# The second group's output product by seven quarter products, feature-major, with sums of weights on GpSimd

## The chip, the cores and the metric

The kernel runs on one core of a Trainium2 chip. Its engines each run their own stream of instructions in order: TensorE (PE in the profile, its loads of stationary operands PEld), VectorE (DVE), ScalarE (ACT), GpSimd (POOL) and SyncE (SP, which issues nearly all transfers between HBM and SBUF). Matrix products go to PSUM, which has eight banks here: five under the tag "acc", three under "mix". The metric is the device time of one execution in microseconds (us), the median of several.

## What is computed

The reference is one layer of a bidirectional encoder, applied to a sample of 1024 tokens and a prompt of 256 with the same weights (D_MODEL 2048):

```python
hn = rms_norm(x, norm_g)
proj = hn @ w_in                                   # conv input, gates z, dt, q, k, v, mq
xbc = silu(centred_dwconv(xbc, conv_w, conv_b))
y = y_forward + y_backward + d_skip * xs           # SSD scans, chunks of 128, both directions
o_ssd = rms_norm over 2 groups of 512 (y * silu(z_ssd)), times ssd_norm_g
o_att = window_attention(q, k, v, sink) * silu(z_att)     # 512 features
o_mem = attention over 256 memory rows * silu(z_mem)      # 512 features
return x + concat([o_ssd, o_att, o_mem]) @ w_out          # 2048 x 2048
```

The last line is what the change is about. All data are float32.

## The kernel before

**Tiles and groups.** The 1280 tokens are ten tiles of 128, in two groups of five (group 0: tiles 0 to 4, group 1: tiles 5 to 9). For one group all activations that a product needs stay in SBUF, turned so that features lie on the partitions: four "quads" `xH0..3` and `xL0..3`, each 4 x 128 features by 640 tokens. Each float32 operand is held as a rounded part (H, or h for weights) and the rest (L, l), and a product is three matmuls: H h, H l and L h.

**Blocks.** `block_tok` computes 512 output columns for five token tiles: for each of 16 slices k of the contraction, SP loads 128 x 512 weights into `wraw` (four buffers), `wsplit` makes `wh` on ACT (L233, or L236 with a scale) and `wl` on DVE (L234 or L237), three buffers each; then come five token tiles x three matmuls (L285 to L287) with the activations stationary and 512 weight columns moving. The last two steps are merged, so that each token tile finishes early and is evacuated while the others run. `block_feat` (L320 to L322) is the other form: weights stationary, 320 tokens moving, the result has features on the partitions. The order of all blocks is written out at the end of the kernel function.

**Lanes.** All other work (attention, memory attention, SSD scans, norms) is written as generators in two queues, `lanes`. After every step of a block, `pump` takes as many steps of each lane as `RATES` says; `need` forces steps that something waits for. The framework then orders the instructions of each engine by priority and readiness, near this order; `high_priority` moves weight splits and evacuations ahead.

**SSD.** `ssd_up` goes through the tiles in ascending order and leaves a part of the result in DRAM; `ssd_down` goes in descending order (7 to 0, later 9 and 8), adds the backward part, multiplies with the gate (L1002), stores the product token-major (L1003, `o_d`), sums its squares on ACT (L1004), and gets the norm's factor on GpSimd (L135, L136, L1010) into `rs_all`.

**Output product.** The quads are refilled with the mixers' results by `refill_o`: quads 0 and 1 (attention, memory) straight from turned copies in DRAM (`oT_d`, by `fill_direct`, L217 to L227), quads 2 and 3 (SSD) by `fill_transposed` (L199 to L211), which loads a token tile, scales it with `rs_all` (L204), turns it by four transposes on TensorE (L207) and splits it (L210, L211). Fills use the three "ch" buffers. Then `block_tok` runs four blocks of 512 columns for group 0 (the lanes finish during the first three; the refill for group 1 runs during the fourth), and four for group 1. The norm's gain per feature rides on the weight splits of the last eight slices (L236, L237). `ev_out` adds the input rows (L416) and stores them (L417). During the last four blocks both lanes are empty.

## Time and profile before

| what | us |
|---|---|
| median of three runs | 1856.73 (1856.13 to 1857.54) |
| the profiled execution | 1857.13 |
| its span | 1855.4 |
| DVE busy in the span | 1068.2 |
| ACT busy | 776.0 |
| GpSimd busy | 84.6 |

The span reaches from the first to the last recorded instruction of one execution; 1.7 us of that execution lie around it. A busy time is the sum over an engine's instructions; matmuls overlap each other, so what one matmul costs in a stream is the distance between two starts, not its duration. A row of a group gives its line, engine, operation, output and inputs, count, then busy us and mean ns of one, then the idle time before it and what ended that. Lines are those of the kernel above.

### The profile page before, as it was taken

To read this page: it belongs to the slowest core of one execution; us is meant where nothing else is said; L and a number is where in the kernel's file an instruction comes from. 1 tells how busy PE (TensorE), PEld (TensorE's weight loads), DVE (VectorE), ACT (ScalarE), POOL (GpSimd) and SP (SyncE) were. 2 spreads that over 40 slices of the span, in tenths; PEclk is the share of its full clock that TensorE was granted. 3 is DMA by queue.
4 is the path that set the end of the run, shared out by engine and by line. 5 is a ranking of instruction groups with operands and counts; after the bars stand their busy time and mean duration, and the time that the engine had idled before them with its cause. 6 is when DMAs were issued, how large, how long until landed. Compare 5 with 4: busy or idle time off the path is not lost.

```text
span 1855.4 us, 28398 instructions
## 1 busy us (share of the span) xinstructions
PE 1847.1 (100%) x10402; PEld 1628.6 (88%) x10402; DVE 1068.2 (58%) x2156; ACT 776.0 (42%) x1753; POOL 84.6 (5%) x147
## 2 busy tenths in 40 slices
PE   9999999999999999999999999999999999999999
PEld 8889999998998889999989988777888888888887
DVE  5434555767456566668786665666885554342222
ACT  6553333434533655324335445544463442322121
POOL 0011001000000000000000000001100000000000
PEclk9999999999999999999999999999999999999999
DMA  8674444443432564533445445467775574554442
GB/s 290 234 234 126 121 148 142 130 123 95 137 128 87 165 200 133 146 96 116 123 140 162 135 142 175 116 214 253 233 218 158 150 228 133 177 173 136 133 123 69
DMA packets 191340, 289.39 MB, mean 156 GB/s; under 512 B 18977, under 2 KB 68193, under 8 KB 191201
## 3 DMA queue, kind: packets, MB, share of 16 engines
q1 hardware_dynamic: 191056, 287.53, 50.2%
q8 instruction: 82, 1.34, 0.3%
q14 instruction: 58, 0.47, 0.1%
q10 hardware_dynamic: 144, 0.06, 0.0%
HBM read 230.59 MB, written 56.92 MB: 155 GB/s over the span
## 4 chain that ended last, share of the span: by engine, by line
PE 94%; DMA 2%; ACT 1%; DVE 1%; issue 1%; SPq 0%; POOL 0%; ACTq 0%; DVEq 0%
PE acc L285 17%; PE acc L287 17%; PE acc L286 17%; PE acc L320 10%; PE acc L321 10%; PE acc L322 10%; PE py L923 2%; PE po L671 1%; PE ppt L661 1%; PE pmo L772 1%; PE pyb L998 1%; PE psc L629 1%; PE pyf L856 1%; PE psc L630 1%; DMA chd<-in_x_turned_dram 1%
## 5 line engine op out<-in xcount | busy, mean ns | idle before, releaser
L285 PE MATMUL acc<-wh,xH 128*128 128x512 f32 (+1 forms) x1568 | 609.6, 389 | 0.6 <-DVE zs L336 0.6
L287 PE MATMUL acc<-wh,xL 128*128 128x512 f32 (+1 forms) x1568 | 597.4, 381 | 0.0
L286 PE MATMUL acc<-wl,xH 128*128 128x512 f32 (+1 forms) x1568 | 596.2, 380 | 0.2 <-DVE wl L234 0.2
L234 DVE TENSOR_TENSOR wl<-wraw,wh 128x512 fp32r<-128x512 f32 (+1 forms) x416 | 278.5, 670 | 383.2 <-ACT wh L233 378.2
L233 ACT ACTIVATE wh<-wraw 128x512 fp32r<-128x512 f32 (+1 forms) x416 | 255.4, 614 | 581.7 <-PE acc L287 294.4
L320 PE MATMUL acc<-xH,wh 128*128 128x320 f32 x1280 | 402.7, 315 | 0.0
L322 PE MATMUL acc<-xH,wl 128*128 128x320 f32 x1280 | 396.1, 309 | 0.0
L321 PE MATMUL acc<-xL,wh 128*128 128x320 f32 x1280 | 395.6, 309 | 0.0
L285 PEld LDWEIGHTS acc<-wh,xH 128*128 128x128 f32 x1568 | 295.0, 188 | 57.7 <-issue 5.6
L286 PEld LDWEIGHTS acc<-wl,xH 128*128 128x128 f32 x1568 | 294.7, 188 | 56.2 <-issue 3.6
L287 PEld LDWEIGHTS acc<-wh,xL 128*128 128x128 f32 x1568 | 294.4, 188 | 55.8 <-issue 0.2
L320 PEld LDWEIGHTS acc<-xH,wh 128*128 128x128 f32 x1280 | 240.4, 188 | 5.4 <-issue 5.0
L321 PEld LDWEIGHTS acc<-xL,wh 128*128 128x128 f32 x1280 | 240.4, 188 | 2.0 <-issue 1.7
L322 PEld LDWEIGHTS acc<-xH,wl 128*128 128x128 f32 x1280 | 240.3, 188 | 0.4 <-issue 0.2
L237 DVE SCALAR_TENSOR_TENSOR wl<-wraw,vec,wh 128x512 fp32r<-128x512 f32 x64 | 48.1, 751 | 139.7 <-ACT wh L236 135.4
L236 ACT ACTIVATE wh<-wraw,vec 128x512 fp32r<-128x512 f32 x64 | 46.3, 723 | 134.1 <-PE acc L287 123.7
L394 DVE SCALAR_TENSOR_TENSOR c<-u,vec,c 128x638 f32<-128x638 f32 (+1 forms) x96 | 84.5, 880 | 0.7
L644 ACT ACTIVATE lg<-lg,nm 128x384 f32<-128x384 f32 (+1 forms) x80 | 45.0, 563 | 46.0 <-DVE nm L638 45.8
L906 ACT ACTIVATE rb<-rb,wj_all 128x128 f32<-128x128 f32 x160 | 52.7, 391 | 25.9 <-DMA rb<-ac 25.9
L227 DVE SCALAR_TENSOR_TENSOR xL<-chd,vec,xH 128x640 fp32r<-128x640 f32 (+1 forms) x48 | 39.7, 838 | 36.5 <-ACT xH L226 35.1
L631 DVE SCALAR_TENSOR_TENSOR lg<-ndist,psc 128x384 f32<-128x384 bf16 (+1 forms) x80 | 38.6, 495 | 27.4 <-PE psc L630 26.9
L906 ACT ACTIVATE rf<-rf,wj_all 128x128 f32<-128x128 f32 x160 | 52.1, 391 | 2.3 <-DMA rf<-ac 2.3
(254 smaller groups left out, 1762.2 us busy)
## 6 DMA issues: line engine op xcount, KB each, us to landing
wraw<-in_w_in_laid_dram SPq DMA_DIRECT2D x288, 256.0 KB, 2.8
wraw<-in_w_out_laid_dram SPq DMA_DIRECT2D x128, 256.0 KB, 2.8
chd<-in_x_turned_dram SPq DMA_DIRECT2D x32, 320.0 KB, 4.6
rf<-ac SPq DMA_DIRECT2D x40, 256.0 KB, 3.8
rb<-ac SPq DMA_DIRECT2D x40, 256.0 KB, 4.0
out_dram<-yt SPq DMA_DIRECT2D x40, 256.0 KB, 3.5
wraw<-in_w_mem_laid_dram SPq DMA_DIRECT2D x32, 256.0 KB, 4.3
xst<-in_x_sample_dram SPq DMA_DIRECT2D x32, 256.0 KB, 4.2
```

Source lines behind the costliest of these rows:

```text
L233: a = A.activation(h, raw, AF.Copy)
L234: b = V.tensor_sub(l, raw, h.bitcast(F32))
L236: a = A.activation(h, raw, AF.Copy, scale=g)
L237: b = V.scalar_tensor_tensor(out=l, in0=raw, scalar=g, in1=h.bitcast(F32), op0=ALU.mult, op1=ALU.subtract)
L285: T.matmul(ps[t][:, :n], sh, h[:, :n], start=(k_ == 0), stop=False)
L286: T.matmul(ps[t][:, :n], sh, l[:, :n], start=False, stop=False)
L287: T.matmul(ps[t][:, :n], sl, h[:, :n], start=False, stop=(k_ == KT - 1))
L320: T.matmul(o, sh, cur["H", q][:, m, c], start=(k == 0), stop=False)
L321: T.matmul(o, sh, cur["L", q][:, m, c], start=False, stop=False)
L322: T.matmul(o, sl, cur["H", q][:, m, c], start=False, stop=(k == KT - 1))
L394: V.scalar_tensor_tensor(out=c[:, :n], in0=u[:, k:k + n], scalar=cw[k], in1=c[:, :n], op0=ALU.mult, op1=ALU.add)
L906: A.activation(r[:, c], r[:, c], AF.Identity, bias=wj_all[:, t, h:h + 1])
```

## The change

Group 0 keeps its four blocks. For group 1, the product (2048 output features x 2048 x 640 tokens) is cut in halves along each of the three directions, and the eight quarter products are replaced by seven, with sums of quarters on both sides (`seven` names for each product which of four weight slices or four weight sums it uses, and which of seven token slices or sums). The result is feature-major and leaves the kernel as a second output of 2048 x 640, turned on the host. In detail:

- `block_pair(u)`, u = 0 to 7, makes 128 features of each half of the output: eight steps k, each with one load of four 128 x 128 weight quarters, four sums of them on GpSimd, two splits (384 and 512 columns), and seven products of three matmuls with 320 moving columns. The seven accumulators take five "acc" banks and two "mix" banks. The last two steps are merged.
- `fill_seven(k)` makes the seven token operands of one slice: two loads, one scaling by the norm's gain (on ACT), four subtractions on GpSimd, and three splits. For k from 4 to 7 they lie where the quads were, once group 0's last block is through with them (`free`).
- `ev_pair` adds the seven products into two output rows of 640 tokens, with nine additions on DVE and one copy on ACT.
- `ssd_down` now scales its product and turns it itself (four transposes, a copy on ACT, a store into `oT_d`), in four more steps of the lane. So `refill_o` takes all four quads by `fill_direct`, with the gain for the SSD quads, and the weight splits of the output product have no scale.
- The tiles that only the earlier stages use lie in two pools (`cl`, `mp`) that are closed ahead of group 0's fourth block, after the lanes have been emptied; the new pool `fin` takes their place.
- The rates of lane 1 are raised for z0, z1, mq, zm and o, that of lane 0 for o.

```diff
-         {'kv': (1.0, 1.0), 'x': (0.9, 1.05), 'q': (1.3, 2.3), 'za': (1.3, 2.3), 'z0': (1.5, 2.4), 'z1': (1.5, 2.4),
-          'mq': (1.5, 1.8), 'zm': (1.5, 1.8), 'o': (1.5, 1.65)})
+         {'kv': (1.0, 1.0), 'x': (0.9, 1.05), 'q': (1.3, 2.3), 'za': (1.3, 2.3), 'z0': (1.5, 2.5), 'z1': (1.5, 2.5),
+          'mq': (1.5, 2.7), 'zm': (1.5, 2.7), 'o': (1.55, 1.9)})
...
-    mp = ctx.enter_context(tc.tile_pool(name="mp", bufs=2))
     sm = ctx.enter_context(tc.tile_pool(name="sm", bufs=2))
+
+    beside = ExitStack()
+    cl = beside.enter_context(tc.tile_pool(name="cl", bufs=1))
+    mp = beside.enter_context(tc.tile_pool(name="mp", bufs=2))
...
+    def lconst(shape, name, dtype=F32):
+        return cl.tile(shape, dtype, tag=name, name=name)
...
-    kT = const([P, 2, 7 * P], "kT", F32R)
-    kL = const([P, 2, 7 * P], "kL", F32R)
-    v_all = const([P, 7, P], "v_all")
-    dt_all = const([P, NT, 32], "dt_all")
-    eacs_all = const([P, NT, 32], "eacs_all")
-    cd_all = const([P, NT, 32], "cd_all")
-    wj_all = const([P, NT, 32], "wj_all")
-    dd_all = const([P, NT, 32], "dd_all")
-    rs_all = const([P, NT, 2], "rs_all")
+    kT = lconst([P, 2, 7 * P], "kT", F32R)
+    kL = lconst([P, 2, 7 * P], "kL", F32R)
...
-    o_d = [[dram([P, 512], f"o{c}_{t}") for c in range(2)] for t in range(NT)]
-    oT_d = [[dram([P, 4, 640], f"oT{c}_{g}") for g in range(2)] for c in range(2)]
+    oT_d = [[dram([P, 4, 640], f"oT{c}_{g}") for g in range(2)] for c in range(4)]
...
-    def fill_transposed(q, i, src, scale=None):
-
-        ch = rp.tile([P, 640], F32, tag="ch", name="ch", bufs=CH)[:, :512]
-        last_load[0] = S.dma_start(ch, src)
-        yield
-        if i == 0:
-            new_quad(q)
-        if scale is not None:
-            V.tensor_scalar(out=ch, in0=ch, scalar1=scale, scalar2=None, op0=ALU.mult)
-        ps = psum("pr")
-        for j in range(4):
-            T.transpose(ps[:, j * P:(j + 1) * P], ch[:, j * P:(j + 1) * P], ident)
-        ps3 = hv(ps, 4)
-        h = cur["H", q][:, :, i * P:(i + 1) * P]
-        A.activation(h, ps3, AF.Copy)
-        V.tensor_sub(cur["L", q][:, :, i * P:(i + 1) * P], ps3, h.bitcast(F32))
-        yield
...
-    def wsplit(raw, h, l, g=None):
-        if g is None:
-            a = A.activation(h, raw, AF.Copy)
-            b = V.tensor_sub(l, raw, h.bitcast(F32))
-        else:
-            a = A.activation(h, raw, AF.Copy, scale=g)
-            b = V.scalar_tensor_tensor(out=l, in0=raw, scalar=g, in1=h.bitcast(F32), op0=ALU.mult,
-                                       op1=ALU.subtract)
+    def wsplit(raw, h, l):
+
+        a = A.activation(h, raw, AF.Copy)
+        b = V.tensor_sub(l, raw, h.bitcast(F32))
...
-        return w_laid(w_out_laid[c], 512, lambda k: vec[:, R_SG + k - 8:R_SG + k - 7] if k >= 8 else None)
+        return w_laid(w_out_laid[c], 512)
...
-            S.dma_start(o_d[t][g], y)
...
-        rsqrt(rs_all[:, t, :], ss, 1.0 / 512, 2)
-        G.tensor_scalar(out=rs_all[:, t, :], in0=rs_all[:, t, :], scalar1=rxh[:, t:t + 1], scalar2=None, op0=ALU.mult)
-        yield
+        rs = sm.tile([P, 2], F32, tag="s2", name="yrs", bufs=4)
+        rsqrt(rs, ss, 1.0 / 512, 2)
+        G.tensor_scalar(out=rs, in0=rs, scalar1=rxh[:, t:t + 1], scalar2=None, op0=ALU.mult)
+        yield
+        yield
+        for g in range(2):
+            y = ld[g][0]
+            V.tensor_scalar(out=y, in0=y, scalar1=rs[:, g:g + 1], scalar2=None, op0=ALU.mult)
+        yield
+        for g in range(2):
+            y = ld[g][0]
+            ps = psum("pr")
+            for j in range(4):
+                T.transpose(ps[:, j * P:(j + 1) * P], y[:, j * P:(j + 1) * P], ident)
+            o = mp.tile([P, 512], F32, tag="rf", name="so", bufs=2)
+            A.activation(o, ps, AF.Copy)
+            S.dma_start(oT_d[2 + g][grp][:, :, ti * P:(ti + 1) * P], hv(o, 4))
+            yield
+    seven = {1: (0, 0, 0), 2: (0, 1, 5), 6: (1, 1, 2), 5: (1, 0, 1), 3: (1, 3, 6), 7: (1, 2, 3), 4: (0, 2, 4)}
+    rows = {}
+    free = [0]
+    def fill_seven(k):
+        q, j = divmod(k, 4)
+        a, b = [rp.tile([P, 640], F32, tag="ch", name=n, bufs=CH) for n in ("ra", "rb_")]
+        S.dma_start(a, oT_d[q][1][:, j, :])
+        S.dma_start(b, oT_d[2 + q][1][:, j, :])
+        yield
+        A.activation(b, b, AF.Copy, scale=vec[:, R_SG + k:R_SG + k + 1])
+        yield
+        a, b = hv(a, 2), hv(b, 2)
+        t = fin.tile([P, 4, 320], F32, tag="tt", name="tt", bufs=2)
+        for i, x, y in ((0, a[:, 1], a[:, 0]), (2, b[:, 1], a[:, 1]), (1, b[:, 1], t[:, 0]), (3, b[:, 0], t[:, 1])):
+            G.tensor_tensor(out=t[:, i], in0=x, in1=y, op=ALU.subtract)
+        yield
+        yield
+        while free[0] < k - 3:
+            yield
+        if k < 4:
+            h, l = [fin.tile([P, 7, 320], F32R, tag=f"{n}{k}", name=n, bufs=1) for n in ("rH", "rL")]
+        else:
+            h, l = [xp.tile([P, 8, 320], F32R, tag=f"x{n}{k - 4}", name=f"r{n}") for n in "HL"]
+        for c, src in ((slice(0, 1), a[:, 0:1]), (slice(5, 7), b), (slice(1, 5), t)):
+            A.activation(h[:, c], src, AF.Copy)
+            V.tensor_sub(l[:, c], src, h[:, c].bitcast(F32))
+        rows[k] = h, l
+        yield
+    def ev_pair(u):
+        r0, r1 = [ev.tile([P, 2, 320], F32, tag=n, name="yr") for n in ("evt", "evu")]
+        w = rp.tile([P, 2, 320], F32, tag="ch", name="yu", bufs=CH)
+        rows_ = [slice(c, c + P) for c in (u * P, D // 2 + u * P)]
+        for r, c in zip((r0, r1), rows_):
+            S.dma_start(r, hv(x_turned[1, c, :], 2))
+        def add(out, ps, x):
+            V.tensor_tensor(out=out, in0=ps, in1=x, op=ALU.add)
+        def f(p, ps):
+            if p == 1:
+                A.activation(w[:, 0], ps, AF.Copy)
+                add(r0[:, 0], ps, r0[:, 0])
+            elif p == 2:
+                add(r0[:, 0], ps, r0[:, 0])
+            elif p == 6:
+                add(w[:, 0], ps, w[:, 0])
+            elif p == 5:
+                add(w[:, 1], ps, w[:, 0])
+                add(r0[:, 1], w[:, 1], r0[:, 1])
+                add(r1, w, r1)
+            elif p == 3:
+                add(r0[:, 1], ps, r0[:, 1])
+                S.dma_start(hv(y_turned[rows_[0], :], 2), r0)
+            elif p == 7:
+                add(r1, ps.unsqueeze(1).broadcast_to([P, 2, 320]), r1)
+                S.dma_start(y_turned[rows_[1], 320:], r1[:, 1])
+            else:
+                add(r1[:, 0], ps, r1[:, 0])
+                S.dma_start(y_turned[rows_[1], :320], r1[:, 0])
+        return f
+    def block_pair(u):
+        ps = {p: (acc.tile([P, 512], F32, tag="acc", name="acc") if i < 5 else psum("accm"))[:, :320]
+              for i, p in enumerate(seven)}
+        parts = {}
+        for k in range(8):
+            raw = wp.tile([P, 512], F32, tag="wraw", name="wraw", bufs=RB)
+            S.dma_start(raw, w_out_pairs[u, k])
+            with tc.high_priority(offset=HP[2]):
+                sums = fin.tile([P, 512], F32, tag="ws", name="ws", bufs=3)
+                w11, w12, w22, w21 = [raw[:, i * P:(i + 1) * P] for i in range(4)]
+                s1, s2, s3, s4 = [sums[:, i * P:(i + 1) * P] for i in range(4)]
+                for o, x, y, op in ((s1, w21, w22, ALU.add), (s3, w11, w21, ALU.subtract),
+                                    (s2, s1, w11, ALU.subtract), (s4, w12, s2, ALU.subtract)):
+                    G.tensor_tensor(out=o, in0=x, in1=y, op=op)
+                h = [wp.tile([P, 512], F32R, tag="wh", name="wh", bufs=WB)[:, :384],
+                     fin.tile([P, 512], F32R, tag="sh", name="sh", bufs=3)]
+                l = [wp.tile([P, 512], F32R, tag="wl", name="wl", bufs=WB)[:, :384],
+                     fin.tile([P, 512], F32R, tag="sl", name="sl", bufs=3)]
+                wsplit(raw[:, :384], h[0], l[0])
+                wsplit(sums, h[1], l[1])
+            parts[k] = h, l
+            if k == 2:
+                evac = ev_pair(u)
+            if k == 6:
+                continue
+            ks = (6, 7) if k == 7 else (k,)
+            need(fill_seven, [x for x in ks if x not in rows])
+            for p, (i, m, c) in seven.items():
+                for k_ in ks:
+                    h, l = [x[i][:, m * P:(m + 1) * P] for x in parts[k_]]
+                    xh, xl = [x[:, c] for x in rows[k_]]
+                    T.matmul(ps[p], h, xh, start=(k_ == 0), stop=False)
+                    T.matmul(ps[p], h, xl, start=False, stop=False)
+                    T.matmul(ps[p], l, xh, start=False, stop=(k_ == 7))
+                if k == 7:
+                    with tc.high_priority(offset=HP[0]):
+                        evac(p, ps[p])
+            yield k
...
-            if q < 2:
-                return [part(fill_direct, q, j, oT_d[q][grp][:, j, :]) for j in range(4)]
-            ts = [grp * 5 + i for i in range(5)]
-            return [part(fill_transposed, q, i, o_d[t][q - 2], scale=rs_all[:, t, q - 2:q - 1])
-                    for i, t in enumerate(ts)]
+            return [part(fill_direct, q, j, oT_d[q][grp][:, j, :],
+                         gain=None if q < 2 else vec[:, R_SG + 4 * (q - 2) + j:R_SG + 4 * (q - 2) + j + 1])
+                    for j in range(4)]
...
-        tok("o", w_out_rows(c), ev_out(0, c * 512), grp=1)
-    tok("o", w_out_rows(3), ev_out(0, 1536), refill_o(1), grp=1)
-    for c in range(4):
-        tok("o", w_out_rows(c), ev_out(5, c * 512), grp=1)
+        tok("o", w_out_rows(c), ev_out(c * 512), grp=1)
+    for x in lanes:
+        while x:
+            step(x)
+    beside.close()
+    fin = ctx.enter_context(tc.tile_pool(name="fin", bufs=2))
+    queue(0, fill_seven, range(8))
+    for k in block_tok(w_out_rows(3), 5, ev_out(1536)):
+        free[0] = (k + 1) // 4
+        pump((2.5, 0))
+    for u in range(8):
+        for _ in block_pair(u):
+            pump((2.5, 0))
...
+    w = _np.concatenate([att, w[1536:], w[:1024]]).reshape(2, 8, P, 2, 8, P)
+    inputs['w_out_pairs'] = _np.stack([w[0, :, :, 0], w[1, :, :, 0], w[1, :, :, 1], w[0, :, :, 1]]).transpose(3, 1, 2, 0, 4).reshape(8, 8, P, 512)
...
-    return tuple(r.results[0][f"out_{i}_dram"] for i in range(len(_OUTS)))
+    y = _np.concatenate([r.results[0]["out_0_dram"], r.results[0]["out_1_dram"].T])
+    return y[None, 1024:], y[None, :1024]
```

(Among the constants, all that only the earlier stages use go to `lconst`, as the two shown; `rs_all` is gone.)

61 lines of the change are left out of this document (33 added, 28 removed).

## The prediction

> **What bounds the kernel now.** I began with the page's first and fourth parts, busy time by engine and the chain that ended last, and then looked only at the stretch that the change rewrites.
>
> ```profile
> span 1855.4 us, 28398 instructions
> PE 1847.1 (100%) x10402; PEld 1628.6 (88%) x10402; DVE 1068.2 (58%) x2156; ACT 776.0 (42%) x1753; POOL 84.6 (5%) x147
> PE 94%; DMA 2%; ACT 1%; DVE 1%; issue 1%; SPq 0%; POOL 0%; ACTq 0%; DVEq 0%
> ```
>
> A busy TensorE (PE) can still be one that runs slowly, so the 100% proves little; the 94% of the chain says more. For the second group's output product I read the busy time by stretch, and the DVE's timeline, where the first output addition (L416) of each 512-column block marks its end.
>
> ```profile
> core 0: us, PE busy (x) PEld busy (x) DVE busy (x) ACT busy (x) POOL busy (x), PEclk, DMA share, GB/s
> 1689.00:1743.40 54.40, 54.40 (x242) 45.06 (x241) 14.83 (x22) 10.87 (x17) 0.00 (x0) 1.00 0.40 125
> ```
>
> ```profile
> 1683.00 0.69 DVE L416 TENSOR_TENSOR yt<-acc,yt 128x512 f32<-128x512 f32 x1
> 1737.40 0.69 DVE L416 TENSOR_TENSOR yt<-acc,yt 128x512 f32<-128x512 f32 x1
> 1791.80 0.69 DVE L416 TENSOR_TENSOR yt<-acc,yt 128x512 f32<-128x512 f32 x1
> ```
>
> The blocks are 54.40 us apart to the last digit. A block is 16 steps x 5 token tiles x 3 matmuls = 240, so one 512-column matmul costs 54.40 / 240 = 0.2267 us, and nothing else shows: VectorE (DVE) works 14.83 us of 54.40, ScalarE (ACT) 10.87, GpSimd (POOL) 0. Four blocks are 960 matmuls, **217.6 us**, limited by TensorE's rate at granted clock 1.00. The weight loads show as busy, but fit beside.
>
> **The change, part by part.** *Matmuls of the second group.* Removed are the 960. Added are 8 blocks x 8 steps x 7 products x 3 = 1344 matmuls of 320 columns, weights stationary. The feature-major blocks (L320 to L322) have that shape already, with a new stationary load for each matmul:
>
> ```profile
> 329.99 0.31 PE L320 MATMUL acc<-xH,wh 128*128 128x320 f32 x1
> ...
> 334.83 0.31 PE L320 MATMUL acc<-xH,wh 128*128 128x320 f32 x1
> ```
>
> ```profile
> 329.85 0.19 PEld L320 LDWEIGHTS acc<-xH,wh 128*128 128x128 f32 x1
> 330.00 0.19 PEld L321 LDWEIGHTS acc<-xL,wh 128*128 128x128 f32 x1
> ```
>
> Between these two starts lie 33 matmuls: 4.84 / 33 = 0.1467 us each; loads of 0.19 us start every 0.15 us, so they overlap. 1344 x 0.1467 = **197.1 us**, and this part is worth 197.1 - 217.6 = **-20.5 us** if the operands come in time. A step lasts 21 x 0.1467 = 3.08 us, a block 24.64.
>
> *GpSimd's sums.* Each of 64 steps adds four 128x128 tensor-tensor sums. The trace has none of that size; the nearest rows are these.
>
> ```profile
> L136 POOL TENSOR_TENSOR rs_all<-rs_all,mhalf 128x2 f32<-128x2 f32 x10 | 7.2, 716 | 0.8
> L1099 POOL TENSOR_SCALAR_AFFINE_SELECT dist<-dist 128x384 f32<-128x384 f32 x1 | 0.5, 509 | 6.5 <-DVE dist L1098 6.5
> L90 POOL TENSOR_SCALAR_AFFINE_SELECT upper<-one 128x128 f32<-128x128 f32 x1 | 0.3, 292 | 0.0
> ```
>
> The affine selects give (509 - 292) / 256 = 0.85 ns an element and 184 ns fixed. Ends: 0.29 us (one input of the right size) and 0.72 (two inputs, but a power). I take 0.40: 184 + 2 x 128 x 0.85, the row of the right size with a second input read after the first. Four are 1.6 us of a 3.08 us step. But GpSimd does not run alone:
>
> ```profile
> 1297.70 0.68 DVE L234 TENSOR_TENSOR wl<-wraw,wh 128x512 fp32r<-128x512 f32 x1
> ```
>
> ```profile
> 1284.36 0.19 POOL L135 TENSOR_SCALAR rs_all<-yss 128x2 f32<-128x2 f32 x1 [11.45 <-ACT zd L1004]
> ...
> 1297.83 0.60 POOL L135 TENSOR_SCALAR rs_all<-yss 128x2 f32<-128x2 f32 x1 [12.09 <-ACT zd L1004]
> ```
>
> The same GpSimd instruction takes 0.19 us alone and 0.60 when a DVE subtraction of two SBUF tensors runs, and ends 0.05 us after it (1298.43 against 1298.38): it was held. Such DVE work per step is the two weight splits, 384 and 512 columns, and an eighth of the two SBUF-only additions (320 and 640):
>
> ```profile
> L234 DVE TENSOR_TENSOR wl<-wraw,wh 128x512 fp32r<-128x512 f32 x384 | 263.9, 688 | 351.5 <-ACT wh L233 346.8 <-DMA yp<-ya 3.5
> L234 DVE TENSOR_TENSOR wl<-wraw,wh 128x288 fp32r<-128x288 f32 x32 | 14.6, 456 | 31.7 <-ACT wh L233 31.4
> L233 ACT ACTIVATE wh<-wraw 128x512 fp32r<-128x512 f32 x384 | 241.2, 629 | 547.4 <-PE acc L287 261.1 <-PE acc L321 167.5 <-issue 99.1
> L346 DVE TENSOR_TENSOR zs<-acc,rbc 128x320 f32<-128x320 f32 x32 | 14.6, 488 | 7.9 <-PE acc L322 7.7
> L224 DVE TENSOR_TENSOR xL<-chd,xH 128x640 fp32r<-128x640 f32 x16 | 12.9, 821 | 9.7 <-ACT xH L223 9.7
> ```
>
> 0.69 + 0.56 (384 columns, between the two rows) + (0.49 + 0.82) / 8 = 1.41 us. Held for all of it, GpSimd needs 1.6 + 1.41 = 3.0 us of 3.08; since the held instruction's fixed part passed during the wait, less. So I cost the sums at **nothing** on the path, hidden behind the step's matmuls, with a thin cover: each 0.1 us of a step over 3.08 costs 64 x 0.1 = 6.4 us.
>
> [...]
>
> *DVE and ACT in this stretch.* A block of DVE is 8 x 1.25 for splits plus nine additions (seven of 0.49, two of 0.82, 5.1 us) = 15.1 of 24.64 us; ACT is 8 x 1.2 + 0.5 = 10. Both hidden. At a block's end two steps' operands are held, so the split for the next block's second step starts 0.44 us before the end and has 3.5 us for some 2.3 us of work, behind up to 1.3 us of additions. Ends: 0, and 1.3 a block if the additions stand wholly in front and nothing is spare. I take 0.2 a block, near the first because 3.5 exceeds 2.3: **+1.6**.
>
> *Second group's rows (fill_seven).* Removed: the 8 direct and 10 turned fills of the old refill. Added: 8 fills, each two loads, one scaling, four GpSimd subtractions of 320 columns (0.73 us each by the above, ends 0.46 and the unmeasured power form), three splits (0.5, 0.8, 1.5 us on DVE). With three "ch" buffers and two per fill, the next fill's second load waits for the first tensor of this one. The load:
>
> ```profile
> chd<-oT SPq DMA_DIRECT2D x16, 320.0 KB, 3.8
> ```
>
> 3.8 + 0.8 scaling + about 1.2 until the tensor is free again = 6 us a fill at best, 11 if the whole chain is serial. The last pair is needed 54.4 + 6 x 3.08 = 73 us after the last first-group block begins; 8 x 6 = 48 fits, 8 x 11 = 88 would be 15 late. Nearer to the buffer count is the 6: **0**. Queued behind a waiting load on SP are weight loads, four buffers (12 us) ahead.
>
> *SSD products turned in the descending pass.* The 80 transposes stay 80, and so do 20 scalings and 20 copies; they move from the refills into the lane, five steps a tile later than the store that ended a tile before. The store of the raw product goes, the store of the turned one comes (20 each), and the first group's refill loads 8 tiles of 320 KB for 10 of 256:
>
> ```profile
> L207 PE MATMUL pr<-ident,ch 128*128 128x128 f32 x80 | 10.7, 273 | 0.0
> L204 DVE TENSOR_SCALAR ch<-ch,rs_all 128x512 f32<-128x512 f32 x20 | 9.7, 483 | 8.8 <-DMA ch<-o 8.8
> L236 ACT ACTIVATE wh<-wraw,vec 128x512 fp32r<-128x512 f32 x64 | 46.3, 723 | 134.1 <-PE acc L287 123.7 <-issue 9.2 <-ACT zd L1004 0.7
> L1010 POOL TENSOR_SCALAR rs_all<-rs_all,rxh 128x2 f32<-128x2 f32 x10 | 5.6, 563 | 1.0
> ```
>
> TensorE's sum does not change. The scaled weight splits (0.72) become plain ones, hidden before and after. New is a wait: a tile's transposes stand on PE behind its scale, that behind GpSimd's 0.2 + 0.72 + 0.56 us. Three steps of the lane, over 3 us of matmuls, lie between; if they did not, ten tiles would cost up to 10 x 1.5. I take 0. On SP the refill's loads of the turned products now stand behind the last tile's store, and weight loads behind them; the quad is first read after eight steps of the first o block, 8 x 3.4 = 27 us on, which covers it (without that cover, one store of some 3.3 us). The denser lane meets a busier DVE in this stretch than in the last one, though it adds no DVE instruction but moves some:
>
> ```profile
> 1300.00:1400.00 100.00, 99.29 (x605) 86.09 (x604) 81.94 (x184) 55.98 (x140) 9.24 (x13) 1.00 0.70 221
> ```
>
> ```profile
> oT<-moT SPq DMA_DIRECT2D x10, 256.0 KB, 3.3
> ```
>
> 82% still hides it: 0. By counting steps per pump, 150 lane steps are left at the first o block, and the raised rates serve 48 x (1.55 + 1.9) = 165, so the new loop that empties the lanes finds nothing, and the pools close without a bare stretch; the new tiles that lie in their place wait for the last memory-attention store (3.3 us), early in a block of 54.4.
>
> *Tail.* Now:
>
> ```profile
> 1851.37 0.24 PE acc L287
> 1851.61 0.02 issue
> 1851.64 0.69 DVE yt L416
> ```
>
> 3.1 us of store follow. After, the last four products' additions arrive every 0.88 us and the fifth product's three (1.8 us) hold the rest up by about 0.7: **+0.5**.
>
> **Sum:** -20.5 + 1.6 + 0.5 = -18.4. The profiled execution took 1857.13 us (span 1855.4 and 1.7 around it), 0.4 above the median of the three runs. So 1838.7 for it, **1838** beside the median.
>
> **The rivals.** *GpSimd becomes the bound, slower.* The place is the four sums; the price is 64 times what a step has over 3.08 us. The 18.4 us are gone at 0.29 us over, which is 3.37 a step: a sum of 0.49 us with full holding. At 0.72, the power's row, a step is 2.88 + 1.41 = 4.3, 1.2 over, and the time 1857 - 18 + 77 = 1916; at 0.55 it is 3.61 and 1873. For it: the held row, and a tensor-tensor form that costs 0.7 us for two elements. Against: that row is a power, and fixed time passes while held. [...] Chance 0.20.
>
> *Part of the gain lost:* sums of 0.42 to 0.49 fully held (up to 18 us), or serial fills (15 us): 1843 to 1853. For it: three buffers for two loads at a time. Against: DVE has 40% free. Chance 0.18.
>
> *The gain all eaten, no difference:* both of these at their middle, 1853 to 1860. Chance 0.04.
>
> *The seven products are bound by weight loads* and not by columns: 1344 x 0.188 = 253 us, 35 slower, about 1892. The load rows above speak against it: 0.02, inside the slower 0.20.
>
> **How the numbers follow.** Forecast, TensorE stays the bound: 1834 to 1843, chance 0.58. Lost in part 0.18, no difference 0.04, slower 0.20. The range runs from 1834, the sum without handover charges and a little off, to 1858: it holds the first two cases and most of the third and leaves the slower case out. A measurement of this kernel tells about 0.2% (3.7 us) from no change, so faster 0.76, same 0.04, slower 0.20.
>
> **What the changed profile would show.** Right: the new matmuls 0.147 us apart through the whole stretch, some 198 us; GpSimd busy (held time counted) under 3 us a step; DVE about 60%. Wrong: PE idle before the step's products with a split waiting for GpSimd; a GpSimd sum above 0.5 us; a stall before the first block's last step, from fills; PE waiting at transposes between 1230 and 1350 us, or in the third o block, where the lanes would not have been empty.

## The result and the profile after

The change made the kernel **slower: 1874.1 us median of four runs (1871.82 to 1877.36) against 1856.87, ratio 1.0094, 95% interval 1.0077 to 1.0112**. The forecast was 1838, so 36 us are to be found. The profiled execution took 1872.92 us.

The head of the page after, then the shares of the chain that ended last:

```profile
span 1871.2 us, 29941 instructions
PE 1838.4 (98%) x10786; PEld 1649.5 (88%) x10786; DVE 1150.8 (61%) x2276; ACT 824.0 (44%) x1857; POOL 261.1 (14%) x435
PE 85%; DVE 5%; DMA 4%; ACT 2%; POOL 2%; issue 2%; SPq 0%; DVEq 0%; ACTq 0%; POOLq 0%
```

TensorE's share of the chain fell from 94% to 85%; DVE, ACT, GpSimd and transfers now hold what it lost. The new matmuls themselves go at the rate that was reckoned, but not everywhere. So the place comes first. One mark that both kernels have is the last output addition of the third 512-column block of group 0 (DVE's timeline; before, then after):

```profile
1575.70 0.69 DVE L416 TENSOR_TENSOR yt<-acc,yt 128x512 f32<-128x512 f32 x1
```

```profile
1593.09 0.69 DVE L393 TENSOR_TENSOR yt<-acc,yt 128x512 f32<-128x512 f32 x1
...
1654.00 0.68 DVE L393 TENSOR_TENSOR yt<-acc,yt 128x512 f32<-128x512 f32 x1
...
1685.49 1.81 DVE L1051 TENSOR_TENSOR yr<-yu,yr 128x320 f32<-128x320 f32 x2
...
1865.28 1.23 DVE L1051 TENSOR_TENSOR yr<-yu,yr 128x320 f32<-128x320 f32 x2
```

The rows of after cut it into three stretches: **S1** up to 1593.09; **S2**, the fourth block (ends 1654.00) and the first pair block up to its fifth product's additions (1685.49), 92.4 us; **S3**, the seven pair blocks from there, 179.8 us.

- S1 is 17.4 us late. Some of that is moved work: all 80 transposes stand ahead of the mark, where before had 40 behind it. Eight of them fill 0.82 us of TensorE (a view below: 1362.66 to 1363.48), so 40 are 4.1 us. **13.3 us are lost.** Between 1200 us and the mark TensorE has 12.1 us of gaps in after and 2.0 in before, so 10.1 of the 13.3 us are gaps.
- Behind S1, 278.1 us against 279.7: only 1.6 us won, where 20.5 for the matmuls and the 4.1 of moved transposes make 24.6. **23 us are missing.**

The waits of TensorE after (us in all, times, longest) name what it stood for:

```profile
PE pr L999 <- DVE yd L993: 6.2, 7, 2.7
PE accm L1108 <- DVE yr L1051: 4.9, 7, 2.0
PE pmt L734 <- DVE mpr L726: 4.4, 4, 2.0
PE acc L264 <- DVE wl L216: 3.8, 3, 2.0
PE acc L1110 <- DVE wl L216: 3.4, 2, 1.9
PE acc L1108 <- ACT wh L215: 1.9, 2, 1.8
```

The first is the turned SSD products and belongs to S1, as does the third (the memory attention). The fourth to sixth stand in S2 (but for 0.3 us), the second in S3, once in each of its seven blocks. None of them names GpSimd, but each split or scale may itself have waited for it. Three readings follow, each with its view.

**S1: a tile's chain.** The timeline of after at the longest of the seven waits (the others are of 0.2 to 1.3 us):

```profile
1356.07 0.68 DVE L978 TENSOR_TENSOR y<-pyb,eacs_all 128x512 f32<-128x512 f32 x1
1356.67 0.81 DVE L207 TENSOR_TENSOR xL<-chd,xH 128x640 fp32r<-128x640 f32 x1
...
1358.74 0.69 DVE L980 TENSOR_TENSOR yd<-yd,zd 128x512 f32<-128x512 f32 x1
...
1359.46 0.72 ACT L981 ACTIVATE zd<-yd,rxh 128x512 f32<-128x512 f32 x1
...
1360.36 0.45 POOL L136 TENSOR_SCALAR yrs<-yss 128x2 f32<-128x2 f32 x1 [15.60 <-ACT zd L981]
...
1360.89 0.70 POOL L137 TENSOR_TENSOR yrs<-yrs,mhalf 128x2 f32<-128x2 f32 x1
1361.70 0.29 POOL L988 TENSOR_SCALAR yrs<-yrs,rxh 128x2 f32<-128x2 f32 x1
1362.03 0.88 DVE L993 TENSOR_SCALAR yd<-yd,yrs 128x512 f32<-128x512 f32 x2 [1.27 <-POOL yrs L988]
...
1362.66 1.07 PE L999 MATMUL pr<-ident,yd 128*128 128x128 f32 x8 [2.67 <-DVE yd L993]
...
1363.48 0.40 PE L298 MATMUL acc<-xH,wh 128*128 128x320 f32 x1
```

From the square on ACT to the transposes are 3.2 us through GpSimd and DVE, and TensorE stood for 2.67 of them with the matmuls of a block behind it. The chain also began late. TensorE's last matmul for this tile (L976) starts at 1353.33, and other matmuls then keep it busy until 1359.99; but the tile's three short DVE instructions (L978 to L980, 0.7 us each) end only at 1359.43, because they stood behind a weight split and shared DVE with the subtractions of the refill (L207).

**S2: the fills wait for output rows.** SP's timeline of after, the second load of each fill (L1021) beside the loads and stores of output rows, which use the same "ch" buffers for tiles 0 and 3:

```profile
1628.68 0.33 SPq L1021 DMA_DIRECT2D rb__17136<-oT  x1
1630.80 0.33 SPq L392 DMA_DIRECT2D yt<-in_x_sample_dram  x1
...
1651.85 0.94 SPq L394 DMA_DIRECT2D out_dram<-yt  x2
1655.07 0.33 SPq L1021 DMA_DIRECT2D rb__17237<-oT  x1
```

Six fills went through, 6 to 9 us apart; the seventh's load, 26 us after the sixth's, was issued when the store of 1651.85 had landed, for which SP stood 2.2 us, and released the buffer that an output row had held since 1630.80. That row waits for its sum until its block ends.

**S3: the order on DVE at a block's end.** DVE's timeline of after between two pair blocks:

```profile
1713.07 1.23 DVE L1051 TENSOR_TENSOR yr<-yu,yr 128x320 f32<-128x320 f32 x2
...
1738.43 1.23 DVE L1051 TENSOR_TENSOR yr<-yu,yr 128x320 f32<-128x320 f32 x2
...
1739.98 0.68 DVE L216 TENSOR_TENSOR sl<-ws,sh 128x512 fp32r<-128x512 f32 x1
1740.73 1.30 DVE L216 TENSOR_TENSOR wl<-wraw,wh 128x384 fp32r<-128x384 f32 x2
1741.95 0.95 DVE L216 TENSOR_TENSOR sl<-ws,sh 128x512 fp32r<-128x512 f32 x1
1742.82 1.34 DVE L1051 TENSOR_TENSOR yr<-accm,yr 128x640 f32<-128x640 f32 x2
```

Four splits were let in front of the last additions, which free the "mix" banks; the next block's seventh product needs one of them, and TensorE waits (its timeline):

```profile
1743.78 0.38 PE L1108 MATMUL accm<-rH,wh 128*128 128x320 f32 x1 [0.47 <-DVE yr L1051]
```

From 1713.07 to 1738.43 a block took 25.36 us, not 24.64. Seven blocks at 0.72 more are 5.0 us; the first handover, with a wait of 2.0 us and matmuls 0.267 us apart behind it, not 0.147 (last section), has the rest of what S3 lost.

### The profile page after: what moved, and what is told of

Read it like the earlier page. It is cut to its first block, busy times and chain, and to the rows that moved or that the text cites. A ratio compares the mean times of both kernels' runs of the same rounds, so it can differ in the third digit from the quotient of the medians.

```text
span 1871.2 us, 29941 instructions
## 1 busy us (share of the span) xinstructions
PE 1838.4 (98%) x10786; PEld 1649.5 (88%) x10786; DVE 1150.8 (61%) x2276; ACT 824.0 (44%) x1857; POOL 261.1 (14%) x435
## 4 chain that ended last, share of the span: by engine, by line
PE 85%; DVE 5%; DMA 4%; ACT 2%; POOL 2%; issue 2%; SPq 0%; DVEq 0%; ACTq 0%; POOLq 0%
PE acc L263 12%; PE acc L265 12%; PE acc L264 12%; PE acc L298 10%; PE acc L299 10%; PE acc L300 10%; PE acc L1110 2%; PE acc L1109 2%; PE acc L1108 2%; PE py L900 2%; PE po L648 1%; PE ppt L638 1%; DVE wl L216 1%; POOL tt L1028 1%; PE pmo L749 1%
## 5 line engine op out<-in xcount | busy, mean ns | idle before, releaser
L216 DVE TENSOR_TENSOR wl<-wraw,wh 128x512 fp32r<-128x512 f32 (+2 forms) x480 | 326.9, 683 | 368.3 <-ACT wh L215 359.3
L215 ACT ACTIVATE wh<-wraw 128x512 fp32r<-128x512 f32 (+2 forms) x480 | 286.8, 600 | 505.2 <-PE acc L265 220.9
L263 PE MATMUL acc<-wh,xH 128*128 128x512 f32 (+1 forms) x1248 | 484.9, 389 | 0.2 <-ACT wh L215 0.2
L264 PE MATMUL acc<-wl,xH 128*128 128x512 f32 (+1 forms) x1248 | 473.4, 379 | 3.9 <-DVE wl L216 3.8
L265 PE MATMUL acc<-wh,xL 128*128 128x512 f32 (+1 forms) x1248 | 474.1, 380 | 0.0
L264 PEld LDWEIGHTS acc<-wl,xH 128*128 128x128 f32 x1248 | 234.9, 188 | 48.2 <-DVE wl L216 5.7
L263 PEld LDWEIGHTS acc<-wh,xH 128*128 128x128 f32 x1248 | 235.2, 188 | 47.3 <-issue 7.1
L265 PEld LDWEIGHTS acc<-wh,xL 128*128 128x128 f32 x1248 | 234.7, 188 | 43.0 <-issue 0.5
L216 DVE TENSOR_TENSOR sl<-ws,sh 128x512 fp32r<-128x512 f32 x64 | 47.7, 746 | 70.3 <-ACT sh L215 70.3
L1090 POOL TENSOR_TENSOR ws<-wraw 128x128 f32<-128x128 f32 x128 | 71.0, 574 | 55.5 <-DMA wraw<-in_w_out_pairs_dram 25.0
```

The lines of the kernel that those rows point to most:

```text
L215: a = A.activation(h, raw, AF.Copy)
L216: b = V.tensor_sub(l, raw, h.bitcast(F32))
L263: T.matmul(ps[t][:, :n], sh, h[:, :n], start=(k_ == 0), stop=False)
L264: T.matmul(ps[t][:, :n], sh, l[:, :n], start=False, stop=False)
L265: T.matmul(ps[t][:, :n], sl, h[:, :n], start=False, stop=(k_ == KT - 1))
L1090: G.tensor_tensor(out=o, in0=x, in1=y, op=op)
```

## The experiments

**Theory A**: the placement loses the time, at three spots: transposes in the lane (S1), fills that share buffers and engines (S2), additions at a block's end (S3). **Rival B**: GpSimd's rate is the bound, and all else follows from it. Each ratio stands beside before on the same chip. The first nine ran on chips where before took 1856.9 to 1857.3 us, the last four on one where it took 1858.0, so differences of medians across that line are uncertain by about 1 us. Stretches are from the same DVE rows as above in each run's own profile.

| kernel | S1 | S2 | S3 | median us | ratio (95%) |
|---|---|---|---|---|---|
| after | 1593.1 | 92.4 | 179.8 | 1874.1 | 1.0094 (1.0077 to 1.0112) |
| own_rows | 1596.4 | 88.2 | 177.8 | 1869.9 | 1.0064 (1.0051 to 1.0077) |
| fills_on_dve | 1595.5 | 84.3 | 179.8 | 1867.4 | 1.0053 (1.0040 to 1.0066) |
| turn_group1_only | 1583.3 | 93.9 | 177.9 | 1863.3 | 1.0029 (1.0018 to 1.0040) |
| no_weight_sums | 1597.5 | 83.8 | 173.5 | 1859.9 | 1.0013 (1.0004 to 1.0022) |
| turn_later | 1589.9 | 92.4 | 179.8 | 1869.5 | 1.0066 (1.0054 to 1.0079) |
| evacuate_first | 1597.0 | 93.4 | 172.6 | 1869.6 | 1.0067 (1.0055 to 1.0080) |
| three_mended | 1581.8 | 85.5 | 177.6 | 1852.9 | 0.9975 (0.9965 to 0.9985) |
| four_mended | 1582.5 | 85.6 | 172.6 | 1847.7 | 0.9949 (0.9935 to 0.9962) |
| mended_no_sums | 1582.2 | 77.7 | 172.6 | 1842.0 | 0.9914 (0.9901 to 0.9928) |
| mended_fills_on_gpsimd | 1582.1 | 89.2 | 172.3 | 1851.5 | 0.9968 (0.9956 to 0.9979) |
| fourth_block_first | 1582.8 | 84.7 | 172.6 | 1847.5 | 0.9944 (0.9930 to 0.9957) |
| last_three_later | 1584.2 | 83.9 | 172.6 | 1848.1 | 0.9950 (0.9938 to 0.9963) |

S1 differs by up to 4.4 us between kernels whose edits lie behind it (own_rows, fills_on_dve, no_weight_sums, evacuate_first against after): the framework orders the whole program anew for each. So an edit is judged by its own stretch, and by the median only where that is far more.

**own_rows**: buffers of their own for the fourth block's output rows.

```diff
-            if t in (0, 3):
+            if t in (0, 3) and c0 == 1536:
+                yt = fin.tile([P, 512], F32, tag="fy", name="yt", bufs=2)
+            elif t in (0, 3):
```

> The output rows of token tiles 0 and 3 of the fourth o block get two buffers of their own in the new pool, and no longer take two of the three ch buffers. Theory A (the seven-fold fills stand behind those rows: the seventh fill's second load is issued at 1655.07 us, when the rows' store has landed, although its buffers' last fill was done near 1638): that load comes some 15 us earlier, the waits in the first block of pairs fall from 11 us to 3 to 6, the time falls by 5 to 10 us from 1874 to 1864 to 1869. Rival B (GpSimd's sums of weights are the bound of the last stage): the first block is as long as before within 2 us and the time stays at 1872 to 1876.

S2 fell by 4.2 us and the median by 4.2, under the expected 5 to 10. The wait for the store is a cause: the first pair block fell from 31.5 to 22.4 us. But the fourth block grew from 60.9 to 65.8: the loads of the seventh and eighth fill now fell into it, and TensorE stood there 3.5 us for weight splits on DVE.

**fills_on_dve**: the fills' subtractions on DVE.

```diff
-            G.tensor_tensor(out=t[:, i], in0=x, in1=y, op=ALU.subtract)
+            V.tensor_tensor(out=t[:, i], in0=x, in1=y, op=ALU.subtract)
```

> The four subtractions of each seven-fold fill are made on DVE instead of GpSimd (about 0.49 us each instead of 1.2). Theory A: a fill's chain gets 3 us shorter, so the fills come every 5 to 6 us instead of 8.4; the waits of the fourth o block (6.5 us) fall by half or more, the first pair block still stands behind the ch buffers; the time falls by 3 to 8 us. Rival B: only GpSimd's load in the first pair block falls, by 10 us of 25, and the later blocks stay; less than 3 us. Rival C (DVE's in-order stream is what delays the weight splits): slower by up to 5 us.

S2 fell by 8.1 and the median by 6.7, though the shared buffers stayed. The fourth block took 55.7 us with no gap on TensorE, though the first six fills came hardly closer (6.9 us apart in the mean, 7.6 in after). So it is not the fills' pace that cost time in that block. What each fill's chain costs on GpSimd shows in two timelines of after, GpSimd's and DVE's:

```profile
1604.54 1.12 POOL L1028 TENSOR_TENSOR tt<-ra 128x320 f32<-128x320 f32 x1
1605.61 1.47 POOL L1028 TENSOR_TENSOR tt<-rb__16854,tt 128x320 f32<-128x320 f32 x1
```

```profile
1608.42 1.49 DVE L1039 TENSOR_TENSOR rL<-tt,rH 128x1280 fp32r<-128x1280 f32 x1 [2.08 <-ACT rH L1038]
1609.83 2.63 DVE L216 TENSOR_TENSOR wl<-wraw,wh 128x512 fp32r<-128x512 f32 x2
```

DVE idled 2.08 us for the rounded sums, for which ACT had waited 3.50 us on GpSimd, and a weight split, which needs none of them, stood behind in DVE's order. TensorE then stood for the split, one of the three of the fourth row of waits (its timeline):

```profile
1611.23 0.50 PE L264 MATMUL acc<-wl,xH 128*128 128x512 f32 x1 [1.52 <-DVE wl L216]
```

**turn_group1_only**: for tiles 0 to 4 the token-major store, the transposing refill and the gain on the weight splits come back; tiles 5 to 9 stay turned in the lane.

```diff
-           'mq': (1.5, 2.7), 'zm': (1.5, 2.7), 'o': (1.55, 1.9)})
+           'mq': (1.5, 2.7), 'zm': (1.5, 1.8), 'o': (1.55, 1.9)})
...
+            if t < 5:
+                S.dma_start(o_d[t][g], y)
...
+        if t < 5:
+            return
...
+            return [part(fill_transposed, q, i, o_d[i][q - 2], scale=rs_all[:, i, q - 2:q - 1]) for i in range(5)]
```

> Token tiles 0 to 4 go the old way again: the product is stored token-major, turned at the refill of the first group, the gain rides on the weight splits of the first group's output product, and the lane's rate in the zm blocks is 1.8 again. Tiles 5 to 9 are turned in the descending pass as in the changed kernel. Theory A (TensorE waits at the transposes for the scale behind GpSimd's three instructions, once per tile): five of the eight waits go, the stretch up to the end of the first o block gets 4 to 7 us shorter, and the time falls as much, to 1867 to 1870. Rival D (the stretch is longer because the lane is denser, whatever stands in it): no more than 2 us.

S1 fell by 9.8 us, the median by 10.8, more than expected. The waits at the transposes fell from 6.2 us to this (waits of TensorE, this kernel):

```profile
PE pr L1027 <- DVE yd L1021: 1.9, 3, 1.2
```

That is 4.3 of the 9.8 us. The waits for the memory attention (4.4 us) are gone from the list as well; they are the likely rest, but no run took them away alone. The edit also takes lane 1's rate in the zm blocks back to 1.8, so for that part rival D, the denser lane, stays open.

**no_weight_sums**: the pair blocks without GpSimd's sums.

```diff
-                for o, x, y, op in ((s1, w21, w22, ALU.add), (s3, w11, w21, ALU.subtract),
-                                    (s2, s1, w11, ALU.subtract), (s4, w12, s2, ALU.subtract)):
-                    G.tensor_tensor(out=o, in0=x, in1=y, op=op)
...
-                wsplit(sums, h[1], l[1])
+                wsplit(raw, h[1], l[1])
```

> The four sums of weight quarters are left out: the second split reads the raw quarters in their place, so GpSimd does nothing per step but the token fills remain, and the products are of other weights. Rival B (the sums on GpSimd are the bound): the pair blocks fall from 25.4 to 24.6 us, the first one to 25 or so, and the time falls by 13 us or more, to 1861 or below. Theory A: the later blocks stay at 25.3 to 25.4, since their wait is for a PSUM bank, the first block gets 2 to 5 us shorter because the token fills have GpSimd to themselves; the time falls by 2 to 6 us.

14.2 us less, which by itself speaks for B: S2 fell by 8.6 and S3 by 6.3. Theory A's forecast for the later blocks (25.3 to 25.4 us) failed: they take 24.79. DVE's order at the block's end is nevertheless the one of after (this kernel's DVE timeline):

```profile
1732.48 0.68 DVE L216 TENSOR_TENSOR sl<-wraw,sh 128x512 fp32r<-128x512 f32 x1
...
1734.73 1.34 DVE L1051 TENSOR_TENSOR yr<-accm,yr 128x640 f32<-128x640 f32 x2
```

The same four splits stand in front of the last additions, but take 2.25 us (1732.48 to 1734.73) instead of 2.84 (1739.98 to 1742.82): beside GpSimd's sums DVE's splits took longer (last section). So S3's loss needs both, the order and the sums. Whether the sums' pace is itself a bound, mended_no_sums shows below.

**turn_later**: three more lane steps between scale and transposes, higher rates to make room.

```diff
-           'mq': (1.5, 2.7), 'zm': (1.5, 2.7), 'o': (1.55, 1.9)})
+           'mq': (1.5, 3.5), 'zm': (1.5, 3.5), 'o': (1.55, 2.1)})
...
+        yield
+        yield
+        yield
```

> The changed kernel with three more empty lane steps between a tile's scaling and its transposes, and lane 1's rates raised so that it keeps pace (3.5 in mq and zm, 2.1 in o). Theory A (the cost is TensorE standing at the transposes, which its order puts right behind the end of GpSimd's three instructions): the waits at the transposes, 6.2 us in seven, fall under 2 us, and the time falls by 4 to 8 us from 1874. Rival D (the old way of the first group was cheaper for another reason: fewer steps, other transfers): less than 2 us, or slower.

The median fell by 4.7, S1 by 3.2 (within the 4.4 by which S1 differs without an edit to it), S2 and S3 not at all. Waits of TensorE in this kernel:

```profile
PE pr L1002 <- DVE yd L993: 2.8, 5, 0.9
```

So distance heals part of the wait, 3.4 of 6.2 us, less than expected (under 2 us were to be left). The transposes' place is a cause of these waits; of what turn_group1_only won it has about a third by S1 and under half by the median.

**three_mended**: own_rows, fills_on_dve and turn_group1_only together.

> The three edits that helped, together: own buffers for the fourth block's output rows, the fills' subtractions on DVE, and tiles 0 to 4 turned the old way. If the first two mend one and the same wait (fills late at the first pair block): 1874 - 11 - 7 = 1856. If they add (fills late for two reasons): 1874 - 11 - 7 - 4 = 1852. If what is left in the first pair block is GpSimd's sums alone, that block is 26 to 27 us from the kernel's fourth o block's end.

1852.9, near the sum of the three medians (1874.1 - 4.2 - 6.7 - 10.8 = 1852.4), but by chance: the stretches do not add. S2 fell by 6.9 us, where own_rows and fills_on_dve alone gave 4.2 and 8.1, so these two mend largely the same loss; S1 fell by 11.3, more than the 9.8 of turn_group1_only. So this run shows one loss in S1 and one in S2, not three separate ones. This kernel is faster than before.

**evacuate_first**: after, with the pair blocks' additions ahead of the weight splits. **four_mended**: three_mended with the same line.

```diff
-                    with tc.high_priority(offset=HP[0]):
+                    with tc.high_priority(offset=300):
                         evac(p, ps[p])
```

> The changed kernel with that priority alone. By DVE's order: seven blocks of 24.7, 1874 - 4 = 1870. By GpSimd's sums: blocks of 25.2 to 25.4, 1873 to 1876.

> As three_mended, and the evacuations of the pair blocks 300 places ahead in priority instead of 30, so that the additions that free a PSUM bank are not behind the next weight splits on DVE. If the 0.7 us of every later pair block is the wait for that bank because of DVE's order: blocks of 24.7 instead of 25.37, 3 to 5 us less than three_mended. If it is GpSimd's sums (blocks of 24.8 without them): the wait moves to the splits, less than 1.5 us.

S3 is 172.6 in both, 24.66 a block, with all of GpSimd's sums in place. The stretch of four_mended over one block, and over nearly seven:

```profile
1692.70:1717.40 24.70, 24.70 (x170) 24.70 (x169) 16.26 (x26) 8.70 (x17) 17.71 (x32) 1.00 0.45 139
1665.00:1835.00 170.00, 170.00 (x1161) 170.00 (x1160) 110.90 (x174) 59.76 (x117) 118.44 (x212) 1.00 0.44 131
```

No gap on TensorE while GpSimd works 17.71 us of 24.70: **B is wrong for the steady blocks.** The order's edit alone takes 7.2 us from S3 against after and 5.0 against three_mended; the medians fell by 4.5 and 5.2 (in evacuate_first S1 came 3.9 later, S2 1.0).

**mended_no_sums** and **mended_fills_on_gpsimd**: four_mended without the sums, and with the fills' subtractions back on GpSimd (edits as above).

> four_mended without the four sums of weight quarters (the second split reads raw quarters, so the products are of other weights). Rival B in a weaker form (GpSimd's sums still cost what no_weight_sums gained on the changed kernel, 14 us): 1834 to 1838. Theory A (the sums bound only where the token fills and the evacuations queue with them): the later blocks are 24.66 in both, the first pair block gains up to 4 us; 1843 to 1848.

> four_mended with the fills' subtractions back on GpSimd. If what matters is how long one fill's chain is (four subtractions of 1.2 us in a row ahead of the splits): 4 to 9 us slower than four_mended, lost in the fourth o block and the first pair block. If the own buffers alone were enough: within 2 us of 1848.

Without the sums, S3 stays at 172.6 and S2 falls from 85.6 to 77.7; the median falls by 5.7 (6.7, each beside before on its own chip). With the fills back, S2 rises by 3.6 and the median by 3.8 (2.8 by the same reckoning). So on the mended kernel GpSimd and DVE cost time only in S2, where fills, sums, splits and additions meet. The stretch there in four_mended, then in mended_no_sums:

```profile
1640.00:1665.00 25.00, 22.27 (x132) 21.59 (x132) 16.07 (x24) 9.72 (x19) 14.97 (x28) 0.86 0.53 164
```

```profile
1640.00:1665.00 25.00, 25.00 (x172) 25.00 (x171) 16.00 (x28) 10.02 (x19) 0.00 (x0) 1.00 0.49 154
```

Forty matmuls more in the same 25 us; four_mended has 2.7 us of gaps there, and a clock of 0.86 for the rest. The windows lie at the same time and not at the same work: without the sums the fourth block had ended 5.8 us earlier, and some of the forty are owed to that, since its matmuls are the longer ones (0.227 us, not 0.147).

**fourth_block_first**: four_mended, the fourth block's additions ahead of the splits. **last_three_later**: that, and two more lane steps ahead of the transposes of tiles 5 to 9 (rates 'mq' 3.1, 'o' 2.0).

```diff
-            V.tensor_add(yt, ps, yt)
+            with tc.high_priority(offset=300 if c0 == 1536 else 0):
+                V.tensor_add(yt, ps, yt)
```

> four_mended with the fourth o block's five output additions 300 places ahead too, since TensorE waits 3.0 us for them at the first pair block behind a fill's subtractions and splits on DVE. If that order is what is left: the stretch from the third o block's end to the first pair block's fall by 3 to 5 us, 1843 to 1845. If DVE is simply full there (fills and two kinds of splits): the wait moves to the splits, within 2 us of 1848.

> As fourth_block_first, and two more lane steps between the scaling and the transposes of tiles 5 to 9, with rates to match (3.1 in mq, 2.0 in o). TensorE still waits 1.7 us at three transposes in four_mended; if those go: 1 to 2 us less than fourth_block_first. If the denser lane costs as much elsewhere: the same or up to 2 us more.

-0.2 and +0.4 against four_mended (-1.2 and -0.6, each beside before on its own chip): neither moves the time by what a measurement can tell. The first edit did not do what it was meant for: it moved only the last of the five additions ahead of one split, the fills' subtractions still stand in front of the others, and TensorE still waits 2.5 us for them (3.0 in four_mended). So whether the rest in S2 is the additions' place in DVE's order stays untested. In the second, the waits at the transposes stayed too (1.9 us, 1.7 in four_mended).

## Why the prediction was wrong, step by step

The sum was -18.4 and the span came to +15.8, 34.2 apart. In S1 lie 13.3. The shortest S2 of all runs is 77.7 (mended_no_sums), so 14.7 of it are lost in after; S3 is 7.2 over 172.6, of which 1.6 were reckoned. That makes 33.6; 0.6 us have no place.

- **Matmuls, -20.5: right.** 170 of 170 us busy in four_mended; 24.66 a block against 24.64.
- **SSD products turned, "I take 0": the first failing step.** It rested on three lane steps, over 3 us of matmuls, between GpSimd's instructions and the transposes, and on "82% still hides it" for DVE. At the longest wait TensorE had 6.7 us of work from the tile's last matmul on, but the tile's DVE instructions, among the refill's, used up 6.1 of them before ACT's square; the chain from there took 3.2 us, and TensorE stood at it 2.67. In all it stood 6.2 us in seven places. The bound written there, 10 x 1.5 us, held the 13.3, but the value was the other end. How much is shown: 9.8 us by turn_group1_only, of which 4.3 are these waits; 3.4 by distance alone. The rest, the memory attention's waits among it, stays argued, not shown.
- **fill_seven, "Nearer to the buffer count is the 6: 0": the second.** The period was 6 to 9 us, between the two ends, and would still have fitted. What failed is that the three buffers were taken as the fills' own: output rows of the same block hold them, and the seventh fill's load came 26 us after the sixth's. A GpSimd subtraction took 0.86 us at best and up to 1.95, against 0.73. A split that stands behind the fill's chain in DVE's order was not counted at all; own_rows and fills_on_dve gave 4.2 and 8.1 us of S2 back, and 6.9 in one kernel with turn_group1_only.
- **Handover, +1.6: mis-sized.** 0.72 a block and some 2 us more at the first, 7.2 for seven, not 0.2 each. All four splits that were let in front of the last additions count, not the free time alone, and beside the sums they take 0.6 us longer. evacuate_first removed it.
- **GpSimd's sums, "nothing", with "a thin cover": right for their pace in the steady blocks, wrong at their beginning and for what they do to DVE.** The group on the page after, all four sums of 64 steps (two of its three forms are in other rows):

```profile
L1090 POOL TENSOR_TENSOR ws<-wraw 128x128 f32<-128x128 f32 x128 | 71.0, 574 | 55.5 <-DMA wraw<-in_w_out_pairs_dram 25.0
```

  With 0.57 us each and 17.7 us of a block's 24.70, a step's four are 2.2 us of 3.08, not the 3.0 reckoned with full holding. The test set there, a sum above 0.5 us, was met and yet proved nothing: in four_mended the sums take 0.56 to 0.60 us each, and TensorE has no gap beside them. In S2, where the fills, splits and additions meet, the sums cost 7.8 us on the mended kernel; in after S3 is 6.3 us longer with them than without, and DVE's four splits ahead of the additions take 2.84 us, not 2.25.
- **The clock was not in the sum.** At two of the four places in S2 where TensorE stood for over 1 us, and at the first handover of S3, slow matmuls followed, at granted clocks of 0.52 to 0.80 (last section).

The slower rival had the sign, and at 0.55 us a sum its time, 1873, is nearly the measured one. Its mechanism was not what happened, and the number is luck: that price lay on every step, and steady steps with the additions in order paid none. The second rival named serial fills and was half the truth. The sign was missed because four small steps were set at or near nothing one by one, each with a bound above it, and the bounds were not added: 15 us for the fills, 15 for the transposes and 10 for the handover are more than twice the gain, the sums left aside.

Mended by the four edits, the change gives 1847.7, and 1847.5 with fourth_block_first, 9.4 and 10.6 us better than before on the same chip. What is missing to 1838 is the 5.7 to 6.7 us of mended_no_sums, the 2.4 us that S1 is still late beside moved work (1582.2 - 1575.7 - 4.1), and about 1 us more.

## What to carry to other kernels

When a stage gets a faster form, price the stage ahead of it too: what prepares its operands now runs beside work that had these buffers and engines to itself. List who else uses each buffer tag that a new load takes, and, in each in-order stream, which unrelated instruction stands behind the new wait. If several steps are set at zero with a bound each, add the bounds before giving a chance to the sign.

## What the runs showed of the chip

**Slow matmuls came behind some short waits and not behind others.** Stretches of after (columns as above, the granted clock third from the end):

```profile
1645.00:1650.00 5.00, 4.95 (x16) 3.44 (x16) 1.42 (x4) 0.91 (x2) 2.70 (x7) 0.68 0.40 105
...
1660.00:1665.00 5.00, 3.11 (x20) 2.58 (x18) 1.96 (x2) 2.43 (x4) 3.32 (x4) 1.00 0.93 297
1665.00:1670.00 5.00, 3.23 (x12) 3.23 (x13) 5.00 (x6) 2.52 (x5) 4.59 (x6) 0.52 0.47 146
1670.00:1675.00 5.00, 5.00 (x30) 5.00 (x28) 1.26 (x3) 1.32 (x2) 5.00 (x9) 0.80 0.35 98
```

and TensorE's timeline in them:

```profile
1666.77 0.63 PE L1110 MATMUL acc<-rH,wl 128*128 128x320 f32 x1 [1.90 <-DVE wl L216]
1667.20 0.47 PE L1108 MATMUL acc<-rH,wh 128*128 128x320 f32 x1
...
1671.73 0.46 PE L1110 MATMUL accm<-rH,wl 128*128 128x320 f32 x1
```

After waits of 1.76 and 1.90 us with two matmuls between them, matmuls stand 0.267 us apart (17 between 1667.20 and 1671.73) instead of 0.147: beside the waits' own length they took some 2 us more. After the single wait of 2.02 us ahead of 1644.62 the 512-column matmuls start 0.42 us apart or more up to 1648.10, not 0.227 (granted clock 0.68 from 1645 to 1650); after that of 2.03 us ahead of 1691.51 the 320-column ones stand 0.267 us apart again (12 between 1692.67 and 1695.87, granted clock 0.75 from 1690 to 1695). After waits of 2.67 us (ahead of 1362.66), 2.03 (1532.74), 1.52 (1611.23) and 1.48 (1677.46) the matmuls kept their full rate, at granted clock 1.00. So the length of a single wait does not tell the two kinds apart: the longest ahead of slow matmuls here was 2.03 us, and one of 2.67 had none behind it. What does stays open.

**DVE's splits took longer beside GpSimd's sums.** I had reckoned only GpSimd as held. DVE's splits beside the sums and without them (groups by shape from 1700 to 1830 us, after and no_weight_sums):

```profile
L216 DVE TENSOR_TENSOR sl<-ws,sh 128x512 fp32r<-128x512 f32 x42 | 31.4, 746 | 48.8 <-ACT sh L215 48.8
L216 DVE TENSOR_TENSOR wl<-wraw,wh 128x384 fp32r<-128x384 f32 x41 | 26.7, 661 | 1.1
```

```profile
L216 DVE TENSOR_TENSOR sl<-wraw,sh 128x512 fp32r<-128x512 f32 x41 | 28.3, 691 | 51.3 <-ACT sh L215 50.6
L216 DVE TENSOR_TENSOR wl<-wraw,wh 128x384 fp32r<-128x384 f32 x42 | 22.8, 554 | 0.1
```

55 and 107 ns more for each, some 0.16 us a step: dear where TensorE waits for DVE already, as at the block's end in S3 of after. In four_mended they take 112 and 170 ns more than in mended_no_sums in the same window (802 against 690, 721 against 551), hidden in its steady blocks, where TensorE has no gap.
